# A delta-rule recurrence over two groups of heads: where the filling products stand, and when the second group starts

## The chip, the cores and the metric

The kernel runs on one core of a Trainium2 chip. A core has a matrix engine (TensorE, PE in the profile), a vector engine (VectorE, DVE), a scalar engine (ScalarE, ACT), GpSimd (POOL) and SyncE (SP), which issues transfers. Each engine works off its own instructions in their order; semaphores tie them together. Weights and intermediates come from device memory into on-chip memory (SBUF) by 16 transfer engines (DMA), and products accumulate in PSUM. The metric is the device time of one execution in microseconds; less is better. The kernel before takes 1333.0 us, the median of three runs (1328.92 to 1334.01).

## The reference

Two layers of width 1024 over 512 positions, each with a gated feed-forward part behind it. Layer 0 is a gated MLP; layer 1, where the change lies, is RWKV-7 time mixing with 16 heads of 64. Cut to what matters:

```
xr, xw, xk, xv, xa, xg = (h + (token_shift(h) - h) * mu[i] for i in range(6))
r, k, v = xr @ w_r, xk @ w_k, xv @ w_v
w = -softplus(-(w0 + tanh(xw @ w1) @ w2)) - 0.5
a = sigmoid(a0 + (xa @ a1) @ a2)
g = sigmoid(xg @ g1) @ g2
# kk: k * k_k normalised by head;  k = k * (1 + (a - 1) * k_a)
# per head, state S (64 x 64), for t = 0..511:
S_t = S_{t-1} diag(exp(-exp(w_t))) + (S_{t-1} (-kk_t)) (kk_t * a_t)^T + v_t k_t^T
y_t = S_t r_t
y = group_norm(y) * ln_w + ln_b + (sum(r * k * r_k)) * v
out = (y * g) @ w_o
```

## The kernel before

Matrix products are done to float32 accuracy with three matmuls: each operand is split into a rounded part and a rest (ACT rounds, DVE subtracts), and `mm3` (L282 to L284) multiplies high by high, high by low and low by high. One of these matmuls with 512 columns is called a product below; a block of 128 output columns is 24 of them (8 slices of the contraction, 3 each).

**The stage of pairs.** The 16 heads are 8 pairs (0 to 7) of two. For each pair, `pairs` computes decay, operands and, in `products`, the 64 x 64 matrices of the 8 chunks of 64 positions, and writes them to device memory (`std`, `btd`). The value projection is a generator, `projections`: for value block m = 0 to 7 it does 24 products, then centres and transposes the result (L788, written to `vtd` at L794) and adds the r-k bonus (L802 on PE, L804 on DVE, L805 on ACT). It is the `fill` of this stage: `weave` runs a main generator and takes `rate` steps of the fill for each step of it. A scheduler then orders each engine's instructions by what they depend on and by these places; its result is a fixed order on each engine.

**The inverse.** Each chunk needs the inverse of a triangular 64 x 64 matrix, made by `invert(g)` for the four pairs of group g at once: four copies into a work tile (L952, on ACT), a transposition (L953), 31 steps of one product and one sum each on DVE (L961, L962), two transpositions (L967, L968), copies on ACT (L972, L990, L992) and small matmuls (L982, L985). `invert(0)` runs beside the last pairs, `invert(1)` from the end of the pairs on and beside the first chunks of the recurrence.

**The recurrence.** `scan(g)` goes through the 8 chunks of group g (pairs 0 to 3 are group 0, pairs 4 to 7 group 1). Before, `scan(0)` runs to its end and then `scan(1)`. One chunk is a chain: PE multiplies the state (tile `vu`) by the chunk's matrices (L1054, L1058), DVE copies the result (`wt`, L1056), PE applies the inverse (L1067), DVE and ACT copy that back (L1068, L1069), PE makes the new state (L1074; L1062 beside it), DVE scales it into the next chunk's `vu` (L1079, two), and PE does the output's last part (L1081). The next chunk's L1054 waits for L1079. Each chunk's data is loaded by `load(g, c)` on SP's queue: `st` (two transfers of 384 KB, L1017), `vu` (two of 64 KB, L1019) and `cbt` (256 KB, L1022). `st`, `cbt` and `vu` each have three buffers before, so that the load of chunk c + 3 waits for chunk c's L1081, the last reader of its `st`.

`finish` normalises two chunks' output (L1097 to L1110) and, every four chunks, multiplies it with the gate (L1123 and the 256-column matmuls before it, L1125) and splits it (L1128, L1129). The gate's factor for a group is loaded and split by `gate_weights` (L1002, L1003; ACT L210, L222, L223; DVE L211, L224). `project` is the output projection, the fill beside `scan(1)`: 96 products for group 0 once its gate is done, then 96 for group 1.

**Queues.** ACT issues the weight transfers (ACTq) in its own order, SP issues the rest. A transfer also waits, on its queue, for a transfer issued some places earlier, since transfers share a few semaphores in turn.

Of the kernel before, what the change touches and what calls it, by code (L numbers as in the profile page):

```python
# [2 lines left out]

# [1 line left out]

# [14 lines left out]
P = 128  # L20
D = 1024
KT = 8
# [3 lines left out]
NCH = T // C  # L26
# [1 line left out]
GN_EPS = 64e-5  # L28
C1 = -0.5 * math.exp(-0.5)

RATES = ((1.9, 2), (1.9, 6, 2.2), (0.8, 2, 2), (0.7, 2), (2, 2))
WB = 4
FIRST0, WAIT, STEPS = 1, 1, (2, 2, 2, 2, 2)
NKEY = 3
BT, SCAN = 1, 3
BANKS = ("mm", "aux", "e", "us")
PARTS = ("wk", "wv")

# [103 lines left out]
class Emit:  # L142
# [558 lines left out]
    def rwkv_main(self, r, ctx, gain):  # L701
        nc, tc, A = self.nc, self.tc, self.A
        V, S, G = nc.vector, nc.scalar, nc.gpsimd
# [8 lines left out]
        def tile_(shape, tag, bufs):  # L712
            return ep.tile(shape, F32, tag=tag, bufs=bufs, name=self.uid(tag))
# [10 lines left out]
        ks, used, done, vdone = {}, set(), set(), set()  # L724
# [211 lines left out]
        def invert(g):  # L936
# [3 lines left out]
            tg = ti[g].rearrange("p i c t -> p (i c) t")  # L940
            Q = [(slice(64 * hd + 32 * b, 64 * hd + 32 * b + 32), slice(32 * b, 32 * b + 32))
                 for hd in range(2) for b in range(2)]
# [4 lines left out]
            x, li, tt = blocks("ix"), blocks("li"), blocks("tt")  # L947
            pr = ip.tile([P, 272], F32, tag="pr", bufs=1, name=self.uid("pr"))
            G.memset(tt, 0.0)
            G.memset(tt.rearrange("p s t -> p (s t)")[:, 0:1024:33], 1.0)  # L950
            for rows, cols in Q:
                S.copy(x[rows], tg[rows, :, cols])  # L952
            V.transpose(li.rearrange("p s t -> p t s"), x.rearrange("p u t -> p t u"))  # L953
            for _ in range(WAIT):
                yield
# [10 lines left out]
            z, y = blocks("ix"), blocks("li")  # L966
# [43 lines left out]

        def load(g, c):
            ps = slice(4 * g, 4 * g + 4)
            st = tile_([P, 4 * 3 * P + P], "st", SCAN)
            bt, vu = tile_([P, 4, 2, C], "cbt", SCAN), tile_([P, 2, 4, C], "vu", SCAN)
            for hd in range(2):
                o = P * (1 - hd)
                nc.sync.dma_start(st[H[hd], o:o + 12 * P], std[g][c, H[hd]].rearrange("p i t -> p (i t)"))  # L1017
            for hd in range(2):
                nc.sync.dma_start(vu[H[1 - hd], hd], vtd[c, H[1 - hd], ps])  # L1019
                if c == 0:  # L1020
                    G.memset(vu[H[hd], hd], 0.0)
            nc.sync.dma_start(bt, btd[c][:, ps])  # L1022
            chunks[g, c] = st, bt, vu

        left, sg = [], []

        def scan(g, late=iter(())):

            ih = [(i, hd) for i in range(4) for hd in range(2)]
            y = None  # L1030
            for c in range(NCH):
                last = c == NCH - 1
                if (g, c) not in chunks:
                    load(g, c)
                st, bt, vu = chunks.pop((g, c))
                if (g, c) != (1, NCH - 1):
                    load(g + last, (c + 1) % NCH)
                if c == 1:
                    gw[g] = gate_weights(g)
                if c % 2 == 0:  # L1040
                    y = tile_([P, 4, 2, C], "y", 3)
                us = self.acc("us").rearrange("p (a i f) -> p a i f", a=2, i=4)
# [117 lines left out]
        def take(gen, n):  # L1160
            for _ in range(n):
                if next(gen, self) is self:
                    return
                yield

        def until(gen, end):
            for _ in gen:
                yield
                if end():
                    return  # L1170
# [5 lines left out]
        inv = invert(0)  # L1176
        for _ in take(inv, FIRST0):
            pass
        self.weave(main, inv, fill, *RATES[1], ktiles=STEPS[1])
        for _ in inv:  # L1180
            pass
        while 3 not in vdone:
# [4 lines left out]
        gw = {}  # L1187
        load(0, 0)
        next(inv)
        self.weave(scan(0), inv, fill, *RATES[2], ktiles=STEPS[2])  # L1190
        for _ in inv:
            pass
        for _ in fill:
            pass
        fill = project()
        self.weave(scan(1, left.pop()), None, fill, *RATES[3], ktiles=STEPS[3])
        self.weave(left.pop(), None, fill, *RATES[4], ktiles=STEPS[4])
        for _ in fill:
            pass
# [70 lines left out]
```

## Time and profile before

| | us |
|---|---|
| runs | 1328.92, 1333.0, 1334.01 (median 1333.0) |
| the profiled execution | 1329.71 |
| its span, first to last instruction | 1327.9 |
| PE busy / DVE / ACT | 1271.5 / 835.3 / 629.7 |
| last matmul before the recurrence ends, first one of it starts | 761.5, 776.2 |
| first and last L1054 (the recurrence) | 776.2 to 908.3 |
| mean granted TensorE clock | 0.975 of full |

A row of the timeline or of a group reads: start, duration, engine, source line, operation, output <- inputs, shape, count, and in brackets how long the engine stood idle before it and what released it. A row of the table by stretch reads: stretch, its length, the busy time of each engine with the number of instructions, then the granted TensorE clock (1.00 is full), the share of the transfer engines in use and GB/s. Matmuls overlap, so a product that lasts 0.39 us takes less from start to start.

### The profile page before, as it was taken

To read this page: it belongs to the slowest core of one execution; us is meant where nothing else is said; L and a number is where in the kernel's file an instruction comes from. 1 tells how busy PE (TensorE), PEld (TensorE's weight loads), DVE (VectorE), ACT (ScalarE), POOL (GpSimd) and SP (SyncE) were. 2 spreads that over 40 slices of the span, in tenths; PEclk is the share of its full clock that TensorE was granted. 3 is DMA by queue.
4 is the path that set the end of the run, shared out by engine and by line. 5 is a ranking of instruction groups with operands and counts; after the bars stand their busy time and mean duration, and the time that the engine had idled before them with its cause. 6 is when DMAs were issued, how large, how long until landed. Compare 5 with 4: busy or idle time off the path is not lost.

```text
span 1327.9 us, 19587 instructions
## 1 busy us (share of the span) xinstructions
PE 1271.5 (96%) x7682; PEld 1028.5 (77%) x7682; DVE 835.3 (63%) x1355; ACT 629.7 (47%) x1072; POOL 109.3 (8%) x116
## 2 busy tenths in 40 slices
PE   8999999999999999999998969798999999999996
PEld 6778888888888888777776646676888888888886
DVE  5565487788785434955678575545687777772223
ACT  5444365555553333666676726322454454442221
POOL 3100200000000001310000001111300000000001
PEclk9999999999999999999988978998999999999998
DMA  7232355555566643246877695871222233222322
GB/s 261 82 112 79 111 157 174 169 165 168 167 186 218 210 135 100 83 144 181 232 239 209 192 228 137 202 177 46 80 96 96 96 100 102 99 92 87 103 88 76
DMA packets 100461, 188.52 MB, mean 142 GB/s; under 512 B 16912, under 2 KB 47760, under 8 KB 100368
## 3 DMA queue, kind: packets, MB, share of 16 engines
q10 hardware_dynamic: 36448, 109.46, 26.3%
q1 hardware_dynamic: 63920, 77.81, 20.5%
q8 instruction: 60, 0.98, 0.3%
q14 instruction: 33, 0.27, 0.1%
HBM read 146.67 MB, written 40.57 MB: 141 GB/s over the span
## 4 chain that ended last, share of the span: by engine, by line
PE 81%; DVE 6%; ACT 3%; DMA 2%; issue 2%; POOL 1%; ACTq 0%; DVEq 0%; POOLq 0%
PE mm L282 9%; PE mm L283 8%; PE mm L284 8%; PE e L282 5%; PE e L283 5%; PE e L284 5%; PE us L282 5%; PE us L284 5%; PE us L283 5%; PE aux L282 5%; PE aux L284 5%; PE aux L283 5%; PE us L1054 1%; DMA vu<-vtd 1%; PE e L1081 1%
## 5 line engine op out<-in xcount | busy, mean ns | idle before, releaser
L210 ACT CAST wh<-w 128x512 fp32r<-128x512 f32 (+1 forms) x361 | 220.3, 612 | 402.5 <-PE mm L283 110.8
L211 DVE TENSOR_TENSOR wl<-w,wh 128x512 fp32r<-128x512 f32 x353 | 243.1, 690 | 185.1 <-ACT wh L210 181.0
L282 PE MATMUL mm<-mxh,wh 128*128 128x512 f32 x392 | 162.5, 415 | 1.8 <-ACT mxh L1128 1.4
L283 PE MATMUL mm<-mxl,wh 128*128 128x512 f32 x392 | 158.2, 404 | 0.3 <-DVE mxl L1129 0.3
L284 PE MATMUL mm<-mxh,wl 128*128 128x512 f32 x392 | 156.6, 399 | 0.3 <-DVE wl L211 0.3
L309 POOL TENSOR_TENSOR ss<-ss,sq 128x512 f32<-128x512 f32 x30 | 40.8, 1360 | 777.3 <-issue 594.9
L282 PEld LDWEIGHTS mm<-mxh,wh 128*128 128x128 f32 x392 | 75.4, 193 | 21.1 <-issue 2.8
L284 PEld LDWEIGHTS mm<-mxh,wl 128*128 128x128 f32 x392 | 75.5, 193 | 17.1 <-issue 0.7
L505 ACT ACTIVATE cv<-z,par 128x512 f32<-128x512 f32 x88 | 71.7, 817 | 35.9 <-DVE z L503 35.9
L283 PEld LDWEIGHTS mm<-mxl,wh 128*128 128x128 f32 x392 | 75.4, 192 | 16.6 <-DVE mxl L1129 1.3
L282 PE MATMUL e<-mxh,wh 128*128 128x512 f32 x216 | 84.5, 391 | 0.0
L282 PE MATMUL us<-mxh,wh 128*128 128x512 f32 (+1 forms) x216 | 84.4, 391 | 0.0
L284 PE MATMUL us<-mxh,wl 128*128 128x512 f32 (+1 forms) x216 | 84.1, 389 | 0.0
L283 PE MATMUL us<-mxl,wh 128*128 128x512 f32 (+1 forms) x216 | 84.1, 389 | 0.0
L283 PE MATMUL e<-mxl,wh 128*128 128x512 f32 x216 | 84.1, 389 | 0.0
L284 PE MATMUL e<-mxh,wl 128*128 128x512 f32 x216 | 84.0, 389 | 0.0
L282 PE MATMUL aux<-mxh,wh 128*128 128x512 f32 x208 | 81.2, 391 | 0.3 <-ACT wh L210 0.3
L506 DVE SCALAR_TENSOR_TENSOR cv<-z,par,cv 128x512 f32<-128x512 f32 x88 | 66.0, 751 | 23.9 <-ACT cv L505 23.9
L284 PE MATMUL aux<-mxh,wl 128*128 128x512 f32 x208 | 81.1, 390 | 0.0
L283 PE MATMUL aux<-mxl,wh 128*128 128x512 f32 x208 | 80.9, 389 | 0.0
L507 DVE SCALAR_TENSOR_TENSOR cv<-z,par,cv 128x512 f32<-128x512 f32 x88 | 66.0, 752 | 2.9
L282 PEld LDWEIGHTS e<-mxh,wh 128*128 128x128 f32 x216 | 40.5, 188 | 8.8 <-issue 0.5
(1070 smaller groups left out, 2607.3 us busy)
## 6 DMA issues: line engine op xcount, KB each, us to landing
w<-in_wup ACTq DMA_DIRECT2D x88, 512.0 KB, 3.5
w<-in_wdn ACTq DMA_DIRECT2D x32, 512.0 KB, 3.5
st<-std SPq DMA_DIRECT2D x32, 384.0 KB, 6.0
std<-lq SPq DMA_DIRECT2D x32, 256.0 KB, 4.0
w<-in_wdn ACTq DMA_DIRECT2D x16, 384.0 KB, 3.2
w<-in_wsu ACTq DMA_DIRECT2D x8, 512.0 KB, 3.5
w<-in_wso ACTq DMA_DIRECT2D x8, 512.0 KB, 3.5
pw<-in_wk SPq DMA_DIRECT2D x16, 256.0 KB, 3.3
```

The costliest lines, as they stand in the source:

```text
L210: nc.scalar.copy(hi[r, :n], src)
L211: (lo_eng or nc.vector).tensor_tensor(lo[r, :n], src, hi[r, :n].bitcast(F32), ALU.subtract)
L282: mm(acc, wh, xh, start=first, stop=False)
L283: mm(acc, wh, xl, start=False, stop=False)
L284: mm(acc, wl, xh, start=False, stop=last)
L309: nc.gpsimd.tensor_tensor(self.ss, self.ss, self.sq, ALU.add)
L505: nc.scalar.activation(c, z[:, 2:], AF.Identity, scale=cw(2, i), bias=self.p("conv_b", l * 44 + i))
L506: nc.vector.scalar_tensor_tensor(c, z[:, 1:T + 1], cw(1, i), c, ALU.mult, ALU.add)
L507: nc.vector.scalar_tensor_tensor(c, z[:, 0:T], cw(0, i), c, ALU.mult, ALU.add)
L1054: nc.tensor.matmul(us[H[hd], 0, i, :], ar(i, hd, 0), vu[:, hd, i, :], start=True, stop=True)
L1081: nc.tensor.matmul(e[H[hd], 0, i, :], pt(i, hd), vu[H[hd], hd, i, :], start=False, stop=True, skip_group_check=True)
```

## The change

Five things are edited. (1) While the last pair is worked on, the fill runs at 0.7 steps instead of 1.9. (2) After the recurrence's first load is issued, `LEAD` = 6 steps of the fill are taken before the first chunk. (3) In `invert(1)` two of the four copies at its head go from ACT to DVE. (4) `gate_weights` is placed behind the instructions of DVE and ACT last issued when chunk 1 begins. (5) When `scan(0)` reaches its chunk 6, the rest of the inverse and of the value projection is emptied, the first load of group 1 is issued, and `scan(0)`'s rest and `scan(1)` take turns, step by step; `finish` of group 0's last two chunks follows in the same chain. `vu` and `cbt` get a fourth buffer, `st` stays at three.

```diff
-RATES = ((1.9, 2), (1.9, 6, 2.2), (0.8, 2, 2), (0.7, 2), (2, 2))
+RATES = ((1.9, 2), (1.9, 6, 2.2), (0.8, 2, 2), (0.7, 2), (2, 2), (0.7, 6, 2.2))
+OVER, LEAD = 6, 6
...
-BT, SCAN = 1, 3
+BT, SCAN = 1, 4
...
-            for rows, cols in Q:
-                S.copy(x[rows], tg[rows, :, cols])
+            for n, (rows, cols) in enumerate(Q):
+                if g == 1 and n % 2 == 0:
+                    V.tensor_copy(x[rows], tg[rows, :, cols])
+                else:
+                    S.copy(x[rows], tg[rows, :, cols])
...
-            st = tile_([P, 4 * 3 * P + P], "st", SCAN)
+            st = tile_([P, 4 * 3 * P + P], "st", SCAN - 1)
...
-        left, sg = [], []
-
-        def scan(g, late=iter(())):
+        left, sg, at = [], [], {0: 0, 1: 0}
+
+        def scan(g):
...
-            y = None
+            y, late = None, iter(())
             for c in range(NCH):
                 last = c == NCH - 1
+                at[g] = c
...
-                if (g, c) != (1, NCH - 1):
-                    load(g + last, (c + 1) % NCH)
+                if not last:
+                    load(g, c + 1)
                 if c == 1:
-                    gw[g] = gate_weights(g)
+                    with ExitStack() as behind:
+                        for eng in (mybir.EngineType.DVE, mybir.EngineType.Activation):
+                            behind.enter_context(tc.issue_after(self.last(eng)))
+                        gw[g] = gate_weights(g)
...
+        def turns(a, b):
+
+            for _ in b:
+                yield
+                if next(a, self) is not self:
+                    yield
+
...
-        self.weave(main, inv, fill, *RATES[1], ktiles=STEPS[1])
+        self.weave(until(main, lambda: KT - 2 in done), inv, fill, *RATES[1], ktiles=STEPS[1])
+        self.weave(main, inv, fill, *RATES[5], ktiles=STEPS[1])
...
         load(0, 0)
         next(inv)
-        self.weave(scan(0), inv, fill, *RATES[2], ktiles=STEPS[2])
+        for _ in range(LEAD):
+            next(fill, None)
+        s0, s1 = scan(0), scan(1)
+        self.weave(until(s0, lambda: at[0] == OVER), inv, fill, *RATES[2], ktiles=STEPS[2])
         for _ in inv:
             pass
         for _ in fill:
             pass
+
+        load(1, 0)
         fill = project()
-        self.weave(scan(1, left.pop()), None, fill, *RATES[3], ktiles=STEPS[3])
+        rest = chain(s0, (x for _ in (0,) for x in left.pop()))
+        self.weave(turns(rest, s1), None, fill, *RATES[3], ktiles=STEPS[3])
         self.weave(left.pop(), None, fill, *RATES[4], ktiles=STEPS[4])
```

The lines of the changed kernel stand 2 to 9 further: L788 is L790, L802 is L804, L1054 is L1063, L1067 is L1076, L1081 is L1090.

The first place is PE between the pairs and the recurrence. Before, the last rows of value block 5 (`mm_6713`), then chunk 0, with value block 6 (`mm_6896`) behind its L1067:

```order
L282 MATMUL mm_6713<-mxh_5870,w_1285_6527 128x512
L283 MATMUL mm_6713<-mxl_5871,w_1285_6527 128x512
L284 MATMUL mm_6713<-mxh_5870,w_1286_6528 128x512
L1054 MATMUL us_6814<-vu_6786,st_6784 64x64
L1058 MATMUL e_6815<-vu_6786,st_6784 64x64
L1054 MATMUL us_6814<-vu_6786,st_6784 64x64 x7
L1058 MATMUL e_6815<-vu_6786,st_6784 64x64 x7
L1067 MATMUL us_6814<-wt_6824,ti_5020 64x64 x8
L282 MATMUL mm_6896<-mxh_5673,wh_6714 128x512
```

Now value block 6 (`mm_6813`) stands in front of chunk 0; its last eight products and the bonus of block 5 (L804):

```order
L804 MATMUL mm_6847<-rt_4363,wb_6845 128x512
L285 MATMUL mm_6813<-mxl_5803,wh_6740 128x512
L286 MATMUL mm_6813<-mxh_5802,wl_6741 128x512
L284 MATMUL mm_6813<-mxh_5815,wh_6740 128x512
L285 MATMUL mm_6813<-mxl_5816,wh_6740 128x512
L286 MATMUL mm_6813<-mxh_5815,wl_6741 128x512
L284 MATMUL mm_6813<-mxh_5870,wh_6740 128x512
L285 MATMUL mm_6813<-mxl_5871,wh_6740 128x512
L286 MATMUL mm_6813<-mxh_5870,wl_6741 128x512
L1063 MATMUL us_6866<-vu_6757,st_6755 64x64
L1067 MATMUL e_6867<-vu_6757,st_6755 64x64
```

All 24 products of block 6, the centring of block 5 (L790, four) and its bonus moved ahead of the first L1063. Ahead of block 5's end PE's order is the one before but for a few swapped neighbours.

The second place is ACT at the gate's factor of group 0. Before, its transfers are issued right behind three of value block 7's weights (`wl_6898` and on), both groups' together:

```order
L778 COPY v_6894<-mm_6713 128x512
L268 DMA wl_6898<-wvd_117 128x512
L268 DMA wh_6901<-wvd_117 128x512
L268 DMA wl_6902<-wvd_117 128x512
L1002 DMA w_1336_6925<-in_g 128x512
L1003 DMA w_1336_6925<-in_g 32x512
L800 ACTIVATE wb_7007<-cst,par 128x128
L1002 DMA w_1443_7828<-in_g 128x512
L210 CAST gwh_6932<-w_1336_6925 128x512
```

Now they stand behind the copy of value block 6 (`v_6946`), and in front of chunk 0's L1078 (before L1069):

```order
L780 COPY v_6946<-mm_6813 128x512
L1007 DMA w_1342_6969<-in_g 128x512
L1008 DMA w_1342_6969<-in_g 32x512
L212 CAST gwh_6976<-w_1342_6969 128x512
L224 CAST gw_6972<-w_1342_6969 32x512
L225 CAST gw_6972<-w_1342_6969 32x512
L1078 COPY vu_6757<-us_6866 64x256
```

The transfers of group 1's factor moved to chunk 0 of group 1.

The third place is PE where group 1 starts. Now chunk 6 of group 0 (`us_7626`) ends, chunk 0 of group 1 (`us_7675`) begins, and chunk 7 of group 0 (`us_7762`) stands inside it:

```order
L1090 MATMUL e_7627<-vu_7508,st_7506 64x64 x8
L1063 MATMUL us_7675<-vu_7658,st_7656 64x64
L1067 MATMUL e_7676<-vu_7658,st_7656 64x64
L1063 MATMUL us_7675<-vu_7658,st_7656 64x64 x7
L1067 MATMUL e_7676<-vu_7658,st_7656 64x64 x7
L1076 MATMUL us_7675<-wt_7685,ti_5021 64x64 x8
L1063 MATMUL us_7762<-vu_7619,st_7617 64x64 x8
L1067 MATMUL e_7763<-vu_7619,st_7617 64x64
L1083 MATMUL e_7676<-vu_7658,cbt_7657 64x64
L1067 MATMUL e_7763<-vu_7619,st_7617 64x64 x4
```

Before, chunk 7's rows all stand ahead of the first of group 1. Now chunk 7's L1090 comes behind L1076 of group 1's chunk 1.

More of the change, by code (lines that the diff above doesn't have):

```diff
@@ L2 @@
 from contextlib import ExitStack
+from itertools import chain
 import numpy as np
```

## The prediction

> **What bounds the kernel now.** I read the page's busy times and clock row first, then the waits, then a table by stretch cut at the recurrence's chunks, then the timeline at its edges.
>
> ```profile
> PE 1271.5 (96%) x7682; PEld 1028.5 (77%) x7682; DVE 835.3 (63%) x1355; ACT 629.7 (47%) x1072; POOL 109.3 (8%) x116
> PEclk9999999999999999999988978998999999999998
> PE us L1054 <- DMA vu<-vtd: 14.7, 1, 14.7
> 761.50:776.20 14.70, 0.00 (x0) 0.02 (x1) 10.49 (x26) 5.21 (x8) 0.61 (x2) 0.58 1.01 227
> 776.20:784.80 8.60, 8.59 (x95) 7.07 (x96) 5.45 (x14) 1.10 (x3) 0.00 (x0) 0.73 0.84 197
> 784.80:793.00 8.20, 8.20 (x101) 5.72 (x97) 6.78 (x17) 3.39 (x9) 0.00 (x0) 1.00 1.07 277
> 793.00:806.67 13.67, 13.18 (x266) 10.17 (x265) 12.52 (x29) 6.45 (x15) 2.95 (x2) 1.00 0.68 170
> 806.67:821.42 14.75, 12.64 (x230) 9.65 (x224) 4.22 (x11) 9.63 (x15) 0.00 (x0) 0.77 0.55 116
> 821.42:828.43 7.01, 6.45 (x108) 4.95 (x107) 2.74 (x8) 5.08 (x11) 1.90 (x2) 1.00 0.56 152
> 828.43:837.01 8.58, 6.74 (x116) 5.89 (x116) 6.03 (x16) 2.53 (x7) 1.02 (x1) 1.00 0.92 222
> 837.01:843.48 6.47, 4.90 (x112) 4.14 (x112) 2.95 (x7) 1.73 (x4) 2.25 (x3) 1.00 0.76 167
> 843.48:847.82 4.34, 3.33 (x73) 2.75 (x69) 2.57 (x7) 1.10 (x3) 0.00 (x0) 1.00 1.02 245
> 847.82:853.40 5.58, 3.85 (x83) 3.18 (x81) 3.01 (x7) 1.73 (x4) 1.64 (x1) 0.93 1.03 223
> 853.40:867.25 13.85, 12.41 (x131) 9.82 (x129) 6.84 (x17) 4.93 (x13) 0.00 (x0) 0.78 0.63 153
> 867.25:881.77 14.52, 14.52 (x222) 11.10 (x221) 8.22 (x19) 3.85 (x8) 2.91 (x2) 1.00 0.74 182
> 881.77:913.30 31.53, 31.53 (x429) 23.97 (x425) 17.64 (x41) 9.58 (x22) 6.43 (x4) 1.00 0.46 119
> 916.30:919.40 3.10, 0.01 (x1) 0.02 (x1) 1.88 (x2) 0.44 (x1) 2.41 (x2) 1.00 0.00 0
> 919.40:923.10 3.70, 3.44 (x20) 3.23 (x21) 2.18 (x6) 0.71 (x2) 0.00 (x0) 0.70 0.46 142
> 923.10:927.60 4.50, 4.24 (x12) 2.87 (x11) 2.03 (x5) 0.71 (x2) 0.20 (x4) 0.50 0.00 0
> ```
>
> PE is the bound almost everywhere, so only what it loses in the recurrence can be won: the stop of 14.7 us, where nothing but the first load runs; the same clock, halved until about 780; chunk 3 (806.67 on); the unfilled chunks from 821 to 853; the stop of 3.1 us behind the last chunk and the halved clock after it. Group 0's chunks begin at 776.20, 784.80, 793.00, 806.67, 821.42, 828.43, 837.01 and 843.48; group 1's 0, 1, 2 and 4 at 847.82, 853.40, 867.25 and 881.77.
>
> **The change, part by part.** I follow the start of a chunk, before and after; a minus is a gain.
>
> *The fill beside the last pair* changes nothing: PE's order there is the old one. Cost 0.
>
> *Six steps in the stop.* Rows of the stop's left edge and inside it:
>
> ```profile
> 757.84 1.12 PE L802 MATMUL mm<-rt,wb 128*128 128x512 f32 x2
> 759.04 0.39 PE L284 MATMUL mm<-mxh,w 128*128 128x512 f32 x1
> 761.11 0.39 PE L284 MATMUL mm<-mxh,w 128*128 128x512 f32 x1
> 741.80 0.33 ACTq L268 DMA_DIRECT2D wl<-wvd  x1
> 762.90 0.45 ACTq L1002 DMA_DIRECT2D w<-in_g  x1
> 763.63 1.14 SPq L1017 DMA_DIRECT2D st<-std  x2
> 770.37 0.62 ACT L210 CAST gwh<-w 128x512 fp32r<-128x512 f32 x1 [5.45 <-DMA w<-in_g]
> ```
>
> Nine products take 2.07 us from start to start, 0.23 each. Block 6's 24 (5.5 us) with one centring and one bonus (about 1.1 each) are 7.7 us of PE at full clock; their weights were issued by 741.80. They run until about 769.5 and cover half of the stop. They do not shorten it: its end is the load. That was issued at 763.63 and landed 12.6 us later, while 227 GB/s x 14.7 us = 3.3 MB moved. The gate's transfers, 2 x 320 KB, leave this stretch; value block 4's write of 256 KB, which stood before it, slides in. That is a net 0.4 MB or 1.7 us; the gate's went on the other queue and ran against the load, so up to 3 us more. I take -3.2: start at 773.0 (bounds 0 and -5).
>
> *The inverse paces chunks 0 to 2.* DVE works 12.52 of 13.67 us there. Rows:
>
> ```profile
> 763.92 2.06 DVE L953 STREAM_TRANSPOSE li<-ix 128x1024 f32<-128x1024 f32 x1 [4.23 <-ACT ix L952]
> 777.84 0.42 DVE L1056 COPY wt<-us 128x256 f32<-128x256 f32 x1 [2.26 <-PE us L1054]
> 804.33 2.02 DVE L968 STREAM_TRANSPOSE li<-tt 128x1024 f32<-128x1024 f32 x1
> 806.38 4.21 ACT L972 COPY ti<-li 32x1024 f32<-32x1024 f32 x4 [1.55 <-DVE li L968]
> 810.60 2.36 ACT L990 COPY tt<-aux 32x512 f32<-32x512 f32 x4
> 819.02 2.34 ACT L992 COPY ti<-aux 32x512 f32<-32x512 f32 x4 [4.08 <-PE aux L985]
> ```
>
> With two copies on DVE and no other work between the rest, L953 can begin at about 758.4, 5.5 us earlier. Before, DVE then stood at L1056 for 2.3 us with the inverse's eleventh step behind it; now L1056 stands nine operations (9 x 0.45 us) later, which DVE fills while the load is on its way. Of this the two bonus sums (2 x 0.69, L804) that now stand ahead are paid back. The gate's factor costs in chunk 0 what the stop hid: its transfer is issued when block 6 ends (769.5), landed 7.5 us after issue before (762.90 to 770.37), and ACT's three casts (3 x 0.62) and DVE's two (2 x 0.68) stand ahead of the copies that chunk 0 needs. Queued behind them are L1069 on ACT, L1068 and the inverse on DVE, and for them PE's L1074. That is about 2 us of standing DVE and 1.4 of casts. Two casts of output weights (2 x 0.68) leave these chunks. In sum 5.5 + 2.3 + 4 - 1.4 - 3.4 + 1.4 = 8.4, less what the chunks' own chain holds up: I take -8.0 at chunk 3, start 798.7 (bounds -2 if the casts wait as long as 9 us, -10).
>
> *Chunk 3* took 15.1 us from L968's end (806.35) to chunk 4. Twelve products leave it. What stays is ACT's chain: 4.21 + 0.75 (L1084) + 2.36 + 0.72 (L805) + 2.34 + 0.37 (L1069), and 1.6 for L1074 and L1079: 12.4. Gain 2.7, so -10.7 at chunk 4. Chunk 4 loses its centring and bonus and becomes an unfilled chunk of 6.47 instead of 7.01: -11.2. Chunk 5 stays. Chunk 6 starts at 825.8.
>
> *The second group's early start.* Its loads set the pace, since `st` has three buffers:
>
> ```profile
> SPq L1017 <- PE e L1081: 36.1, 8, 12.7
> 837.47 0.68 PE L1081 MATMUL e<-vu,st 64*64 64x64 f32 x16
> 838.19 1.08 SPq L1017 DMA_DIRECT2D st<-std  x2
> DMA to landing us min/median/max: 3.3/5.9/10.7
> DMA packets 1798, 4.59 MB, mean 229 GB/s; under 512 B 308, under 2 KB 811, under 8 KB 1796
> ```
>
> A load is issued when L1081 ends (838.15, 838.19); its `vu` follows some 1.8 us later and lands in 5.9 (median): 7.7 us from release to use. The load of group 1's chunk 0 is released by chunk 5's L1081, 0.5 us into chunk 6, so it lands at 8.2 and PE stands 1.7 us behind chunk 6. That of chunk 1 is released by chunk 6's L1081, at 6.3 us: chunk 1 starts 14.0 us after chunk 6 instead of 16.4 (853.40 - 837.01). -2.4, in all -13.6. That of chunk 2 is released by group 0's chunk 7, whose L1081 now stands 2.8 us into group 1's chunk 1: 2.8 + 7.7 = 10.5 us for chunk 1. Chunk 2, unfilled, 6.5. Chunk 3 now holds the gate of group 0: it was in chunk 1 before and took 13.85 us, with 1.4 of standing and a halved clock; I take 12. Sum 29.0 against 28.4 (853.40 to 881.77): -13.0 at chunk 4. By then 14 products of the output projection are done instead of 36: 22 x 0.23 = +5.1, in all -7.9. The bandwidth suffices: a chunk's 1.15 MB at 229 GB/s take 5 us.
>
> *The tail.* Rows there:
>
> ```profile
> 912.65 0.68 PE L1081 MATMUL e<-vu,st 64*64 64x64 f32 x16
> 919.41 0.63 PE L1107 MATMUL aux<-cst,y 128*128 128x128 f32 x4 [3.09 <-DVE y L1103]
> ```
>
> The last output takes 6.1 us from L1081's end to L1107. Before, 12 products (2.8 us) covered it; now 36 do (8.3 us). The stop of 3.1 goes, and the halved clock behind it: 0.30 x 3.7 + 0.50 x 4.5 = 3.4. So -6.5, in all -14.4. If the cover comes late (weights), at most these 6.5 are lost. Chunks 4 to 7 hold 10 or 11 products (2.5 us) beside their own 3.7 of PE, no more than an unfilled chunk's 6.47, so they do not hide everything: +1.
>
> Here a rule of the Trainium skill bears on a row. The row: a stop of 3.1 us is followed by clock 0.50 from 923.10 to 927.60. The page "TensorE: Matmul & The Clock Gate", section "HAM oscillation — how this bites in real kernels", has gaps up to some 3.4 us harmless. By it the tail would give 3.1 and the sum 3.4 less; I go by the row.
>
> **Sum:** -14.4 + 1.0 = -13.4. The profiled execution took 1329.71; with 1316.3 that is 1.0% less. Against the median of 1333.0 it is 1319.6; I say 1320.
>
> **Rivals.**
> 1. *The inverse does not come ahead.* DVE works off its instructions in the order written; if a bonus sum or the gate's casts hold it up, chunk 3 starts where it did, give or take 2. For it: DVE's 12.52 of 13.67 shows that the pace is set there, and the casts' wait is new. Against it: block 6's bonus stands behind products that run in the stop. Left are chunk 3's 3.2, the overlap's and the tail's: -13.4 + 6 = -7.4, or 1325.5.
> 2. *The loads hold the second group.* If they take the 10.7 us of the maximum instead of 5.9, group 1's chunks 0, 1 and 2 come 4.8, 4.8 and 4.8 us later, of which the first is inside the second: -13.4 + 10 = -3, or 1330. For it: 10.7 was measured with other transfers beside it, and group 1's gate and two output weights (1.3 MB) now fall in this stretch. Against it: the median.
> 3. *Slower: the clock.* From chunk 3 to group 1's chunk 3 PE is without filling products for 57 us. The rows of 847.82 and 853.40 show the clock falling to 0.93 and 0.78 when it has been 70% busy for a while. A chunk's chain holds about 3.1 us of PE; at half clock 3.1 more, in nine chunks 28 us: -13.4 + 28 = +14, or 1347 if all of it is halved. It is slower than before once the clock is halved in half of the stretch; with two thirds of it, +5, or 1338. For it: fewer products are left for this stretch than before. Against it: 837 to 848 ran at 1.00 unfilled.
> 4. *More:* the load lands at its minimum and the gate's transfer too: -18, or 1315.
>
> **How the numbers follow.** The forecast has 0.45, the first rival 0.17, the loads 0.15, the clock 0.13, more 0.10. About 0.5% (6.7 us) is what a measurement of this kernel can tell from no change. Faster by more: the forecast but for 0.04 (0.41), 0.09 of the first rival, 0.02 of the loads, the last case: 0.62. Slower: 0.10 of the clock, 0.01 of the loads: 0.11. Within: 0.27. The forecast's own range is 1314 to 1326; with the bounds of the first load, the inverse and the loads it reaches 1311 to 1335.
>
> **What would show it.** Right: the stop at the first L1054 of group 0 is 3 to 4 us with 24 products ahead of it; chunk 3 begins 22 to 26 us after chunk 0 (30.5 before); L1107's last wait is gone. Wrong: L1068 or L1069 of chunk 0 waiting more than 4 us for the gate; waits on `st` or `vu` transfers over 3 us each at group 1's first three chunks; clock under 0.8 for more than 15 us of the unfilled chunks.

## The result, and the profile after

The changed kernel is slower. Over 20 runs of each it takes 1338.55 us (1331.46 to 1342.84) against 1328.1 us before (1322.17 to 1334.01): a ratio of 1.008 (95% interval 1.0065 to 1.0096), about 10 us more. The forecast was 13.4 us less (1320, range 1311 to 1335). The profiled execution of the changed kernel took 1333.33 us (span 1331.5), near the low end of its runs; a second profile, taken later, took 1338.64 (span 1336.8), at the median. Both are used below.

The page of the first profile, the granted clock in 40 slices of the span (tenths):

```profile
PEclk9999999999999999999998986799999999999998
```

It now falls to 0.6 and 0.7 in the 25th and 26th slice, 799 to 866 us: from group 0's chunk 2 to group 1's chunk 2. Before, it was 0.8 and 0.9 there.

The table by stretch of the changed kernel's first profile, cut at the chunks (columns as before: stretch, length, busy time of PE, PEld, DVE, ACT, POOL with counts, granted clock, share of the transfer engines, GB/s). The first row ends at chunk 0 of group 0. Group 1's chunks 0, 1, 2, 3 begin at 842.65, 849.43, 857.72 and 871.61; group 0's chunk 7 stands inside group 1's chunk 0, at 845.66:

```profile
757.00:774.67 17.67, 12.75 (x44) 8.12 (x42) 12.04 (x31) 6.43 (x14) 0.61 (x2) 0.81 0.90 220
774.67:785.50 10.83, 9.52 (x106) 6.88 (x105) 8.75 (x20) 5.32 (x12) 0.00 (x0) 1.00 0.83 210
785.50:793.62 8.12, 8.06 (x115) 6.11 (x114) 6.69 (x20) 2.74 (x6) 0.00 (x0) 1.00 0.91 225
793.62:805.15 11.53, 8.39 (x227) 7.02 (x226) 8.53 (x17) 6.46 (x12) 1.65 (x1) 0.86 0.39 93
805.15:820.44 15.29, 12.42 (x232) 10.71 (x229) 2.81 (x8) 6.29 (x11) 0.00 (x0) 0.50 0.46 106
820.44:826.67 6.23, 4.67 (x99) 4.08 (x97) 2.58 (x7) 1.73 (x4) 1.64 (x1) 0.84 0.81 174
826.67:834.24 7.57, 5.74 (x104) 5.10 (x101) 5.59 (x15) 2.53 (x7) 0.61 (x2) 1.00 0.74 173
834.24:842.65 8.41, 6.91 (x112) 5.99 (x112) 3.64 (x8) 1.73 (x4) 1.64 (x1) 0.61 0.62 141
842.65:849.43 6.78, 6.67 (x134) 6.08 (x133) 3.16 (x10) 1.33 (x4) 0.00 (x0) 0.73 0.75 184
857.72:871.61 13.89, 7.16 (x101) 6.16 (x101) 5.85 (x12) 2.87 (x6) 4.54 (x3) 0.55 0.81 190
871.61:883.51 11.90, 10.26 (x118) 7.80 (x115) 8.19 (x20) 5.43 (x12) 1.27 (x1) 1.00 0.72 179
```

Two rows stand out. Chunk 3 of group 0 (805.15) ran at half clock from end to end, 15.29 us. Chunk 2 of group 1 (857.72) took 13.89 us with only 7.16 of PE in it. The milestones beside the forecast (before and the two profiles after; the forecast moves the old starts by its terms):

| starts at, us | before | forecast | after, first | after, second |
|---|---|---|---|---|
| group 0, chunk 0 | 776.20 | 773.0 | 774.67 | 774.04 |
| group 0, chunk 3 | 806.67 | 798.7 | 805.15 | 806.01 |
| group 0, chunk 4 | 821.42 | 810.7 | 820.44 | 821.15 |
| group 0, chunk 6 | 837.01 | 825.8 | 834.24 | 836.84 |
| group 1, chunk 1 | 853.40 | 839.8 | 849.43 | 851.67 |
| group 1, chunk 2 | 867.25 | 850.3 | 857.72 | 860.49 |
| group 1, chunk 4 | 881.77 | 868.8 | 883.51 | 887.94 |
| end of the span | 1327.9 | 1314.5 | 1331.5 | 1336.8 |

The timeline of the first profile shows where the steps went (start, duration, engine, line, what, and in brackets the idle time before it and its releaser):

```profile
767.71 1.50 ACT L795 COPY vt<-mm 64x256 f32<-64x256 f32 x4 [4.91 <-DMA vtd<-vt]
769.26 2.07 PE L804 MATMUL mm<-rt,wb 128*128 128x512 f32 x2 [3.99 <-ACT vt L795]
771.37 0.69 DVE L806 TENSOR_TENSOR rt<-mm,v 128x512 f32<-128x512 f32 x1 [4.64 <-PE mm L804]
774.67 0.34 PE L1063 MATMUL us<-vu,st 128*64 128x64 f32 x4
774.78 0.34 ACTq L1007 DMA_DIRECT2D w<-in_g  x1
778.08 0.62 ACT L212 CAST gwh<-w 128x512 fp32r<-128x512 f32 x1 [2.71 <-DMA w<-in_g]
798.25 2.00 DVE L973 STREAM_TRANSPOSE li<-tt 128x1024 f32<-128x1024 f32 x1
801.09 0.68 PE L1090 MATMUL e<-vu,st 64*64 64x64 f32 x16 [2.22 <-DVE vu L1088]
801.71 3.52 PE L987 MATMUL aux<-ix,ti 32*32 32x32 f32 x128
812.88 1.16 ACT L997 COPY ti<-aux 32x512 f32<-32x512 f32 x2 [4.03 <-PE aux L990]
851.07 0.60 ACTq L237 DMA_DIRECT2D w<-in_wo  x1
861.37 1.14 ACT L212 CAST wh<-w 128x512 fp32r<-128x512 f32 x2 [6.85 <-DMA w<-in_wo]
862.02 0.69 DVE L213 TENSOR_TENSOR wl<-w,wh 128x512 fp32r<-128x512 f32 x1 [6.53 <-ACT wh L212]
866.34 0.42 DVE L1065 COPY wt<-us 128x256 f32<-128x256 f32 x1
866.82 1.12 PE L1076 MATMUL us<-wt,ti 64*64 64x64 f32 x16 [5.76 <-DVE wt L1065]
```

Read from the top. The six steps ran into a stop of their own: the bonus needs the transposed values `vt`, whose only buffer is free when the write to `vtd` has landed. The eight products behind that wait also ran at half clock, 0.43 us from start to start instead of 0.23. So block 6 ended at 774.7, not at 769.5, and the gate factor behind it was issued at 774.78, its casts inside chunk 0. Chunk 0's first product (L1063) follows block 6 without idle time: it did not wait for its load any more. The `vu` transfers of that load, issued at 765.66 and 766.30, had landed by 771.3; the view of the tile `vu` for these two says

```profile
DMA to landing us min/median/max: 5.0/5.2/5.5
```

and for the same two in the kernel before 10.0 to 10.7. The inverse did come ahead (L973 ended at 800.2; its counterpart L968 before at 806.35), though DVE had stood 4.64 us in front of block 5's bonus sum (L806). But PE then stood for want of other work and resumed at half clock: the inverse's products L987 took 3.52 us, and ACT waited 4.03 us for the next ones (L990). At the bottom is what the forecast did not have. The first output weights (`w<-in_wo`) are now issued at 851.07, behind group 1's gate factor. In the timeline of the kernel before they stand 75 us earlier:

```profile
775.72 0.39 ACTq L235 DMA_DIRECT2D w<-in_wo  x1
```

Now they landed 10 us after their issue, and their casts stand on ACT and DVE in front of chunk 2's `wt` copy, so that PE waited 5.76 us for that copy. Between the two, DVE does the normalisation of group 0 (862.6 to 866.3, 1.75 us of it a wait for GpSimd), which had also been held up behind the cast.

Two theories came from this. **W**: the late output weights are the main loss. **C**: the halved clock in chunks with no products beside them is. A third, **G**, puts part on the gate factor's casts inside chunk 0.

### The profile page after: what moved, and what is told of

It reads as the page before. It is cut to its first block, busy times and chain, and to the rows that moved or that the text cites. A ratio compares the mean times of both kernels' runs of the same rounds, so it can differ in the third digit from the quotient of the medians.

```text
span 1331.5 us, 19591 instructions
## 1 busy us (share of the span) xinstructions
PE 1272.6 (96%) x7682; PEld 1032.0 (78%) x7682; DVE 838.4 (63%) x1357; ACT 627.8 (47%) x1070; POOL 109.9 (8%) x116
## 4 chain that ended last, share of the span: by engine, by line
PE 82%; DVE 5%; DMA 3%; ACT 3%; issue 2%; POOL 1%; ACTq 1%; SPq 0%; DVEq 0%; POOLq 0%
PE mm L284 8%; PE mm L285 8%; PE mm L286 8%; PE e L284 6%; PE e L286 6%; PE e L285 5%; PE us L284 5%; PE us L286 5%; PE us L285 5%; PE aux L284 5%; PE aux L286 5%; PE aux L285 5%; PE e L1083 1%; DMA w<-in_wo 1%; PE us L1063 1%
## 5 line engine op out<-in xcount | busy, mean ns | idle before, releaser
L284 PE MATMUL mm<-mxh,wh 128*128 128x512 f32 x392 | 159.8, 408 | 1.3 <-DVE h L1165 1.3
```

The costliest lines, as they stand in the source:

```text
L284: mm(acc, wh, xh, start=first, stop=False)
```

## The experiments

All were timed in five rounds beside the kernel before (median 1328.96 to 1329.37 us on these chips). Ratios are against it.

| kernel | us | ratio, 95% interval |
|---|---|---|
| the change, again | 1338.74 | 1.0072 (1.0046 to 1.0099) |
| group 1's gate factor early | 1342.51 | 1.0095 (1.0068 to 1.0123) |
| no lead | 1329.62 | 1.0008 (0.9988 to 1.0028) |
| no overlap | 1331.06 | 1.0016 (0.9997 to 1.0035) |
| more small products | 1335.22 | 1.0039 (1.0022 to 1.0056) |
| output weights staged | 1332.67 | 1.0026 (1.0007 to 1.0044) |
| no lead, weights staged | 1324.79 | 0.9969 (0.9948 to 0.9990) |
| no lead, no overlap | 1322.54 | 0.9945 (0.9921 to 0.9969) |
| before, with the two copies on DVE | 1329.50 | 1.0006 (0.9981 to 1.0031) |
| lead, no overlap, gate factor first | 1329.76 | 1.0009 (0.9990 to 1.0028) |
| lead, no overlap, fill spread | 1329.34 | 0.9994 (0.9975 to 1.0013) |
| lead, no overlap, both | 1326.83 | 0.9988 (0.9973 to 1.0003) |

### Group 1's gate factor early

```diff
-                        for eng in (mybir.EngineType.DVE, mybir.EngineType.Activation):
+                        for eng in (mybir.EngineType.DVE, mybir.EngineType.Activation) if g == 0 else ():
```

> The changed kernel with only the second group's gate factor no longer placed behind chunk 1; the first group's stays late. The order then puts the first output weights' transfer (w<-in_wo) back into chunk 0 of group 0, instead of chunk 1 of group 1 (851.07 us in the changed kernel). Theory W (the late output weights are the main loss): the stop of 5.76 us in front of L1076 in group 1's chunk 2 goes, that chunk takes 6 to 8 us instead of 13.9, and the time falls by 7 to 10 us against the changed kernel, to within 3 us of the kernel before. Theory C (the main loss is the halved clock in the unfilled chunks of group 0): only the stop itself moves, 2 to 5 us, and the clock rows of group 0's chunks 3 and 6 stay at 0.5 and 0.6. Rival (loads): the transfers that come early again compete with the first load, group 0's chunk 0 starts 2 to 4 us later and nothing is won.

Measured 1342.51 us: slower still. Its table by stretch at group 0's chunks 1 and 2 and at group 1's chunk 2, and its timeline on ACT:

```profile
784.55:799.54 14.99, 10.00 (x106) 7.06 (x105) 7.17 (x17) 4.84 (x10) 2.04 (x2) 0.69 0.65 159
799.54:815.65 16.11, 11.62 (x234) 10.02 (x233) 9.80 (x20) 8.59 (x15) 2.13 (x2) 0.71 0.79 185
871.14:879.49 8.35, 6.81 (x101) 5.71 (x100) 3.85 (x11) 0.37 (x1) 1.64 (x1) 0.70 0.87 187
```

```profile
789.07 1.14 ACT L212 CAST wh<-w 128x512 fp32r<-128x512 f32 x2 [5.62 <-DMA w<-in_wo]
```

Group 1's chunk 2 fell from 13.89 to 8.35, near the 6 to 8 of theory W. But the same cast, waiting 5.62 us for the same transfer, now stood in group 0's chunk 1, which took 14.99 us instead of 8.12; chunk 2 took 16.11 instead of 11.53. The mechanism of W was right and this cure wrong: the stop goes wherever the cast is put in front of the chain before its transfer has landed.

### No lead; no overlap; more small products

The first takes `OVER, LEAD = 6, 0` and the old rate beside the last pair. The second gives back the old order of the groups. The third adds repeated products that nobody reads:

```diff
+                    for _ in range(3 if (g == 0 and c > 1) or (g == 1 and c < 3) else 0):
+                        for i, hd in ih:
+                            nc.tensor.matmul(us[H[hd], 0, i, :], ar(i, hd, 0), vu[:, hd, i, :], start=True, stop=True)
                     nvu = chunks[g, c + 1][2]
```

> The changed kernel with LEAD = 0 and the old rate beside the last pair: value block 6 stands beside chunks 0 to 2 again, all else as changed. Theory C: moving those products ahead won almost nothing, since the chunks that lost them ran at half clock (0.50 over the whole of chunk 3); the time stays within 2 us of the changed kernel or falls by up to 4, and the clock in chunk 3 rises from 0.50 to 0.75 or more. The prediction's own sum (products in the stop are worth 3 us of start and 5 of the inverse): the time rises by 6 to 8. Theory W makes no difference here: the stop in group 1's chunk 2 stays.

> The changed kernel without the overlap: group 1 starts when group 0 is through, its first load is issued in chunk 7 of group 0 as before, and group 0's last normalisation runs beside group 1's chunks. All else as changed. If the overlap is what costs (22 products fewer by group 1's chunk 4, a stop there), the time falls by 4 us or more against the changed kernel. If the overlap pays by its tail (forecast 6.5 us, of which the halved clock behind the stop of 3.1 us is 3.4), the time rises by 2 to 6: the stop of 3 us in front of the last L1116 is back. Theory W expects the stop for the output weights to shrink but not to vanish, since their transfer is still behind the second gate factor.

> The changed kernel with 24 more small products (64 columns) in each of eight chunks (2 to 6 of group 0, 0 to 2 of group 1), behind L1083, where PE waits 0.5 to 2.2 us for DVE; they repeat L1063 into a half that nobody reads any more. Theory C: PE is kept busy, the clock rows of group 0's chunks 3 to 6 rise from 0.50 to 0.84 towards 1, and the time falls by 5 to 10 us although PE does 8 x 0.9 = 7 us more work. Theory W: the clock is not what matters, the products cost what does not fit in the waits, 0 to 4 us more. If the clock does not depend on these gaps, it stays at 0.5 in chunk 3 and the time rises by 2 to 7.

Without the lead, 1329.62: 9 us less than the change, against the 6 to 8 more that the prediction's sum gives and the at most 4 less of theory C. Chunks 2 and 3 in its table by stretch:

```profile
792.53:806.17 13.64, 12.76 (x267) 10.09 (x266) 9.94 (x22) 7.54 (x14) 1.65 (x1) 1.00 0.33 80
806.17:816.99 10.82, 10.82 (x241) 8.03 (x240) 3.34 (x9) 7.48 (x14) 0.00 (x0) 1.00 0.50 123
```

Chunk 3 has 9 products more than in the changed kernel, and takes 4.5 us less: at clock 1.00 instead of 0.50.

Without the overlap, 1331.06: 7.5 us less than the change. Its chunks 0 and 3 (the code up to chunk 6 is that of the changed kernel), and ACT in chunk 0:

```profile
775.10:790.73 15.63, 12.30 (x106) 9.04 (x105) 8.80 (x20) 5.41 (x12) 0.00 (x0) 0.78 0.93 227
810.92:825.91 14.99, 12.15 (x233) 10.55 (x229) 2.81 (x8) 6.18 (x11) 0.00 (x0) 0.50 0.45 103
```

```profile
780.53 0.62 ACT L212 CAST gwh<-w 128x512 fp32r<-128x512 f32 x1 [4.74 <-DMA w<-in_g]
```

Chunk 3 is at 0.50 again, 15 us. Chunk 0 took 15.63 us here and 10.83 in the changed kernel's first profile, with the gate factor's wait at 4.74 instead of 2.71 and clock 0.78 instead of 1.00.

The added products made the kernel 3.3 us faster than the change, although PE does more: a set takes 1.62 us at full clock, eight of them 13 us, not the 7 of the expectation. Chunks 2 and 3 in its table, then from its timeline one set of the added products (L1088 here; the profile lists each as two records) and the inverse's products:

```profile
794.77:805.13 10.36, 8.49 (x275) 7.15 (x274) 8.67 (x17) 5.17 (x11) 1.65 (x1) 1.00 0.24 55
805.13:819.12 13.99, 12.74 (x282) 11.43 (x276) 2.81 (x8) 7.58 (x12) 0.00 (x0) 0.64 0.68 152
```

```profile
799.80 1.62 PE L1088 MATMUL us<-vu,st 128*64 128x64 f32 x47
802.99 2.21 PE L987 MATMUL aux<-ix,ti 32*32 32x32 f32 x128
```

Chunk 2 now ran at full clock to its end and L987 took 2.21 us instead of 3.52; chunks 4 to 6 ran at 1.00. Chunk 3 still fell to 0.64. With two sets of added products chunks 2 and 3 together took 24.4 us; in the changed kernel, without them, they took 26.8. So theory C holds in its direction: work added to PE raised the clock and shortened the stretch. It does not hold in full, since chunk 3 did not come near 1.00 and the whole gain is 3.3 us and not the 5 to 10 expected.

### The change again; output weights staged; lead and overlap both out

The first is unaltered. The staging issues the first two weight transfers in chunks 2 and 3 of group 0 and casts them two chunks later. The last has only the two copies and the late gate factors left.

```diff
+STAGE = {2: 0, 3: 1, 4: 0, 5: 1}
...
+                if g == 0 and c in STAGE:
+                    with ExitStack() as behind:
+                        for eng in (mybir.EngineType.DVE, mybir.EngineType.Activation):
+                            behind.enter_context(tc.issue_after(self.last(eng)))
+                        next(half[STAGE[c]])
```

> The changed kernel unaltered, for a second profile beside the next three: its first profile (1333.33 us, clock 0.972) lies 5 us below the median of its 20 runs (1338.55). Theory C (halved clock): a run near the median shows more of the unfilled chunks at clock 0.5, the work before chunk 0 unchanged. Theory G (the gate factor's casts in chunk 0 wait for a transfer whose landing varies): a run near the median shows chunk 0 lasting 13 to 16 us instead of 10.8, with ACT waiting over 4 us for w<-in_g, as the profile of the kernel without the overlap did (15.6 us).

> The changed kernel with the first two transfers of output weights issued in chunks 2 and 3 of group 0 and their casts placed two chunks later (4 and 5), so that none stands in front of group 1's chunks 0 to 2. Theory W (late weights cost the stop of 5.8 us and the halved clock behind it): group 1's chunk 2 takes 6 to 9 us instead of 13.9, and the time falls by 5 to 8 us against the changed kernel. Rival (transfers): the weights now collide with group 0's loads, whose chunks 4 to 6 get 3 to 6 us longer, and nothing is won, as with the gate factor placed early, where the stop only moved to group 0's chunk 1. Theory C keeps chunk 3 at clock 0.5 in this kernel too.

> The same staging of the output weights, and no products ahead of chunk 0 (LEAD = 0, the old rate beside the last pair). If the two losses are separate (the unfilled chunks at half clock, 9 us by the kernel without the lead, and the late weights, 5 to 8), this is 4 to 7 us faster than the kernel before: 1322 to 1325. If the weights' transfers are only moved into another stop, it stays at 1329 to 1332.

> Neither the products ahead nor the overlap: only the two copies of the inverse on DVE and the late gate factors are left of the change. The prediction gave the copies some 5 us and charged 3.4 for the gate. If these two parts do nothing by themselves, the time is the one before within 2 us, and the whole loss of the changed kernel needs lead and overlap together (1329.6 with the overlap alone, 1331.1 with the lead alone, 1338.6 with both). If the copies pay as predicted, it is 3 to 5 us faster than before. If the gate factor's late place is the loss, it is 3 us or more slower.

The change again: 1338.74. Its profile, at the median, has chunk 0 at 11.75 us, so the gate factor's wait is not what sets this run apart from the first. Chunks 4 to 6 ran at 0.75, 0.84 and 0.76 (0.84, 1.00 and 0.61 in the first), and group 1's chunk 3 at 0.83 instead of 1.00: more unfilled work at low clock, as C expects, with chunk 3 as before:

```profile
806.01:821.15 15.14, 12.12 (x232) 10.52 (x228) 2.81 (x8) 6.18 (x11) 0.00 (x0) 0.50 0.46 103
```

Staged: 1332.67, 6 us less than the change. Chunk 3 of group 0 and chunk 2 of group 1:

```profile
807.59:823.09 15.50, 12.44 (x233) 10.70 (x229) 2.81 (x8) 6.15 (x11) 0.00 (x0) 0.50 0.55 133
862.52:870.77 8.25, 7.27 (x100) 6.03 (x100) 3.14 (x9) 0.37 (x1) 1.62 (x1) 0.67 0.82 182
```

Chunk 2 of group 1 is down from 13.9 to 8.25 us and chunk 3 of group 0 untouched: W, shown alone. Together with no lead, 1324.79. Without lead and overlap, 1322.54, the fastest of all. Even with its weights staged the overlap was not seen to pay; the two intervals overlap. So the four kernels with and without the two parts are

| us | no lead | lead |
|---|---|---|
| groups one after the other | 1322.5 | 1331.1 |
| groups overlapped | 1329.6 | 1338.6 |

The lead costs 8.5 to 9 us and the overlap 7 to 7.5, each whether the other is there or not. Within the intervals they simply add: my expectation that the loss might need both is wrong. What is left of the change, copies and late gate factors, gains 7 us. Chunk 3 of that kernel:

```profile
806.84:817.66 10.82, 10.82 (x241) 8.03 (x240) 3.34 (x9) 7.47 (x14) 0.00 (x0) 1.00 0.48 118
```

### The copies alone; three repairs of the lead

```diff
-            for rows, cols in Q:
-                S.copy(x[rows], tg[rows, :, cols])
+            for n, (rows, cols) in enumerate(Q):
+                if g == 1 and n % 2 == 0:
+                    V.tensor_copy(x[rows], tg[rows, :, cols])
+                else:
+                    S.copy(x[rows], tg[rows, :, cols])
```

That is the first, on the kernel before. The other three stand on the kernel with the lead and without the overlap: `gate_weights(0)` ahead of the six steps; the fill's rate beside the first chunks 0.4 instead of 0.8; both.

> The kernel before with only the two copies at the head of the second inverse moved from ACT to DVE. Without lead and overlap the change's other two parts together were 6.4 us faster than before (1322.5). If the copies carry it (the inverse starts some 5 us earlier, so chunk 3 does not wait for it), this kernel is 4 to 7 us faster than before: 1322 to 1325. If the late gate factors carry it, it is within 2 us of before.

> The kernel with the lead and without the overlap (1331.1), with the first group's gate factor taken in front of the six steps instead of behind them; its other input (sg) stays in chunk 1. Its transfer is then issued some 10 us earlier than 775 us, and its casts no longer stand inside chunk 0. Theory G (with the lead, chunk 0 lasts 10.8 to 15.8 us instead of 9.1 to 10.4 since the casts wait there): chunk 0 takes 8 to 10 us and the time falls by 3 to 5 us, to 1326 to 1328; chunk 3 stays at clock 0.5 and 15 us. Theory C (all of the lead's loss is the unfilled chunks 2 and 3): within 2 us of 1331. Rival: the transfer now competes with the first load, chunk 0 starts 2 to 4 us later, and nothing is won.

> The kernel with the lead and without the overlap (1331.1), with the fill beside the first chunks at half the rate (0.4 instead of 0.8 steps), so that the last value block's 24 products stand 12, 0, 12, 6 in group 0's chunks 0 to 3 (with some of them counted from the block before) instead of 15, 9, 0, 0. Theory C (the lead's loss comes from chunks 2 and 3 having nothing beside them, so that the clock halves): chunk 3 runs at clock 0.8 or more and takes 11 to 12 us instead of 15, and the time falls by 3 to 6 us. Theory G: chunk 0 stays as long as it was, the time falls by at most 2 us. If the clock there does not depend on the fill, chunk 3 stays at 0.5.

> Both at once: the gate factor in front of the six steps and the last block's products spread over chunks 0 to 3. If the lead's loss of 8.5 us (1331.1 against 1322.5 without the lead) is chunk 0's casts and the unfilled chunks 2 and 3, nearly all of it is back: 1321 to 1325. If it stays above 1328, something else in the lead costs, such as the stop of 4 us for the buffer of the transposed values.

The copies alone do nothing that can be told from the noise (1329.50). Chunk 3 of that kernel, and PE in it:

```profile
798.98:815.40 16.42, 12.35 (x230) 9.07 (x225) 3.41 (x9) 8.29 (x15) 0.00 (x0) 0.81 0.50 110
```

```profile
803.76 0.21 PE L1065 MATMUL e<-vu,cst 64*64 64x64 f32 x1 [2.97 <-issue]
```

So it takes the gate factors' late place to bring chunk 3 to 10.8 us; whether that place does it without the copies was not run. That place also moves the output weights' first transfers and casts out of group 0's chunks; which of the two it is was not separated.

Of the repairs, spreading brought chunk 3 to 12.08 us at clock 0.86, the gate factor first brought chunk 0 to 10.52 us; each gained under 2 us where 3 to 6 were expected, which the intervals do not tell from nothing. With the gate factor first, chunks 2 and 3 stayed slow: 13.48 and 15.02 us at clock 0.72 and 0.73. Both together gained 4.2 us of the lead's 8.5, not nearly all of it as expected. From chunk 0 to chunk 4 that kernel took 42.2 us, like the kernels without the lead (41.7 to 43.2); the four unrepaired ones with it took 45.8 to 51.5. Then the repaired kernel lost again in group 1's chunk 1, 17.49 us against 14.64 in the kernel without lead and overlap, where a cast of output weights stood ahead of ACT's half of the `vu` copy:

```profile
855.93 0.62 ACT L212 CAST wh<-w 128x512 fp32r<-128x512 f32 x1 [7.51 <-DMA w<-in_wo]
856.57 0.37 ACT L1081 COPY vu<-us 64x256 f32<-64x256 f32 x1
856.99 1.11 PE L1086 MATMUL e<-vu,cbt 128*64 128x64 f32 x14 [4.06 <-ACT vu L1081]
```

## Why the prediction was wrong, step by step

**The fill beside the last pair** was costed at nothing; no run tells it apart from the six steps.

**The six steps, -3.2 at chunk 0's start: failed.** The load, on which the prediction built this term, landed by 771.3, earlier than the 773.0 it forecast. But "they run until about 769.5" was wrong: block 5's bonus waited 3.99 us for a buffer, whose write was issued at 759.34 and landed 8 us later, and the rest of block 6 ran at half clock. So block 6 itself set the start, at 774.67, and the gate factor's issue moved to 774.78 and its wait and casts into chunk 0. The second profile shows the same (a wait of 4.09 us, the load there by 771.6, the start at 774.04). The four profiles of kernels with the lead (the change twice, no overlap, staged) start chunk 0 at 774.67, 774.04, 775.10 and 771.60, mean 773.9; the three without it (no lead; no lead with weights staged; neither lead nor overlap) at 775.26, 768.76 and 774.65, mean 772.9. Nothing was won there. With the lead, chunk 0 takes 10.83, 11.75, 15.63 and 15.79 us (mean 13.5); without it 9.07, 10.41 and 10.33 (mean 9.9). That is 3.6 us. Of the four, the two long ones ran at clock 0.78; the three without the lead ran at 0.60 to 0.69, behind their stop, and were still shorter.

**The inverse, -8.0 at chunk 3: half right, and the half that counts was wrong.** The inverse ended 6.1 us earlier than before, but not by the six steps: with the lead it ended at 800.25, 800.55, 805.47 and 802.13, without it at 801.96, 796.81 and 802.63. The prediction charged the bonus sums that now stand ahead with their length, 2 x 0.69; the wait in front of one was 4.64 us. That is what the first rival (0.17) named, and its sign came true: chunk 3 started at 805.15 and 806.01, not at 798.7 (806.67 before). Its price, 6 us, did not cover what came behind. And "the inverse paces chunks 0 to 2" was read from DVE's 12.52 of 13.67 us alone: in the same row PE was busy 13.18. PE's products were the pace as much as the inverse. With those products gone, chunk 2 took 12.0 us (mean of the four) instead of 13.7 (mean of the three without the lead): 1.7 won.

**Chunk 3, -2.7: the largest miss.** The prediction counted from the end of the inverse's last transposition to chunk 4: 15.1 us before, 12.4 forecast. It took 20.2 and 20.6 us in the two profiles of the change, and 15.0 to 15.2 in the three kernels without the lead that keep the late gate factors (the copies alone took 20.0). The 12.4 added up ACT's copies and had no term for ACT's waits for PE, though its own row of L992 shows one of 4.08 us; it took for granted that these go with the twelve products. They did not (4.03 us for L990), while PE did that work at half clock. Chunk 3 took 15.29, 15.14, 14.99 and 15.50 us with the lead, all four at clock 0.50, and 10.82, 10.82 and 10.94 without it, all three at 1.00, with 9 products more. The lead took away what kept PE busy. From chunk 0 to chunk 4 this makes 3.6 - 0.1 - 1.7 + 4.4 = 6.2 us; with 1.0 at the start and 0.8 in chunks 4 and 5 it is 8.0 of the 8.5 measured. The kernels with more small products and with the fill spread show that the clock has a large part in it: work added to that stretch makes it shorter.

The third rival named this mechanism, with 0.13; it looked for the clock after long low use, and took the unfilled chunks at 1.00 (837 to 848) as evidence against. Its 1338, for two thirds of the stretch halved, is close to the 1338.55 measured; that is in part chance, since chunk 0's 3.6 us and the stop for the late weights are not in its sum. In the event the drop came after short waits: PE stood 0.85 and 2.22 us in chunk 2, and nearly everything from 801 to 822 ran at half clock.

**The overlap, -2.4 and +5.1: a term was missing.** The prediction credited "two casts of output weights leave these chunks" and did not ask where they went; its second rival named the weights as bytes in this stretch only. In the order of ACT's rows, the transfers of group 1's factor moving to chunk 0 of group 1 also moved the output weights, which come behind them. Price: group 1's chunk 2 takes 13.9 us instead of 8.25 once staged, 5.6 us; staging gains 6 us in the change and, without the lead, 4.8. The forecast gave this chunk 6.5 us. Without the overlap the weights come as late (853.05 in the kernel with neither part), but the chunk they meet there takes 14.64 us against 13.85 before: in the overlap they fall on a chunk with no products beside it. What is left of the overlap's cost once they are staged stays open.

**The tail, -6.5 + 1: too large.** From group 1's chunk 4 to the end the five profiles with the overlap (the change twice, no lead, both staged) take 448.4 us on the mean, four without it (before, copies alone, no overlap, neither) 445.3. With 22 products, 5.1 us, more to do that is a gain of 2.0, not 5.5. The stop of 3.1 us did go, but in all five profiles three waits of PE of 0.91, 0.43 and 0.57 us came in its place. And the halved clock behind the stop, 3.4 us in the profile of before, is smaller elsewhere. The kernel without lead and overlap, around its stop (which ends at 918.84):

```profile
915.80:918.80 3.00, 0.00 (x0) 0.00 (x0) 1.85 (x2) 0.38 (x1) 2.35 (x2) 1.00 0.00 0
918.80:921.50 2.70, 2.66 (x15) 2.69 (x16) 1.86 (x6) 0.00 (x0) 0.00 (x0) 0.59 0.62 193
921.50:926.00 4.50, 3.85 (x18) 3.08 (x18) 2.48 (x6) 1.42 (x4) 0.20 (x4) 0.87 0.00 0
```

There it is 0.41 x 2.7 + 0.13 x 4.5 = 1.7 us. That leaves 3.1 - 1.9 + 1.7 = 2.9 us of the 6.5, before the prediction's own +1. So the term was sized on one execution of a thing that varies from run to run, and without the waits that the new order brings.

**The sum.** The forecast was -13.4. Measured: lead +8.5, overlap +7.1, copies and late gate factors -6.8 against the kernel before; together +8.8, and the change as a whole +9.4 in the same rounds. So the two parts that carried the forecast cost time, and the small edits paid.

The Trainium skill, page "TensorE: Matmul & The Clock Gate", section "HAM oscillation — how this bites in real kernels", gives the rule to leave no idle gaps of over some 3.4 us, and the prediction read it as calling shorter ones harmless; chunk 3 at 0.50 behind waits of 0.85 and 2.22 us says otherwise, and the measurement decides. The next section of that page, "A second HAM failure mode: psum-queue depth-cycling", has frequent small idles between groups of matmuls make the clock swing. The trace agrees with it in outline: behind such waits the clock was 0.84, 1.00 and 0.61 in chunks 4 to 6 of the first profile. The prediction should have weighed that rule beside the other.

## What to carry to other kernels

Filling work beside a chain of small dependent steps does more than use idle time: it holds the clock at which the chain itself runs. Before moving it into a stop, look at what the chain will be without it, and read PE's busy time in the row as well as that of the engine that seems to set the pace. When an instruction is moved, look at what now comes behind it on the same queue and the same buffers: here a gate factor that was moved took the output weights with it, by 75 us, and a cast that waits for a transfer stops every copy queued behind it.

## What the runs showed of the hardware

The granted clock explains much of the spread between runs of one kernel. Over the 20 runs of the changed kernel, time and mean granted clock have a correlation of -0.86, and 0.01 of clock is worth 8 us; over three sets of 29 to 35 runs of the kernel before it is -0.90 to -0.96 and 8.3 to 9.7 us. The mean clock is 0.9695 in the first and 0.977 in the second, so by the first slope some 6 of the 10 us between them go with the clock.

A halved clock outlasts its cause. In the changed kernel's first profile, cut inside chunks 2 to 4:

```profile
797.00:801.00 4.00, 1.01 (x16) 0.73 (x16) 3.97 (x7) 2.56 (x6) 0.58 (x1) 1.00 0.08 20
801.00:805.00 4.00, 3.91 (x144) 3.84 (x144) 1.42 (x3) 3.46 (x6) 1.06 (x1) 0.61 1.00 239
805.00:810.00 5.00, 3.61 (x58) 3.12 (x54) 0.42 (x1) 3.76 (x6) 0.00 (x0) 0.50 1.04 237
810.00:816.00 6.00, 6.00 (x147) 5.31 (x148) 1.13 (x4) 1.74 (x4) 0.00 (x0) 0.50 0.33 75
816.00:822.40 6.40, 4.92 (x72) 4.21 (x71) 1.68 (x4) 2.29 (x5) 0.00 (x0) 0.50 0.14 17
822.40:826.00 3.60, 2.10 (x50) 1.69 (x48) 2.12 (x5) 0.37 (x1) 1.04 (x1) 1.00 0.95 226
```

The idle stretch is 797 to 801, at full clock. The work behind it pays: 20 us at or near 0.50, among them 6.00 us in which PE was busy without a break. Then, with PE busy 2.10 of 3.60 us, the clock is back at 1.00. What decides when it returns stays open.
